# Three couples of chunks per feed-forward stage by seven block products instead of two, with two weight sums made by adding DMA loads and weight units split whole

## The chip, the cores and the metric

One core of a Trainium2 chip runs the whole program. The metric is the device time of one execution in microseconds (us). The engines are called as in the profile: PE (matrix products), PEld (its weight loads), DVE (VectorE), ACT (ScalarE), POOL (GpSimd), SP (which issues DMAs). A change of this kernel's time by less than 0.2% can't be told from none.

## The reference

A decoder trunk of two layers on 256 tokens of 1024 channels in float32. Each layer is a feed-forward step, a mixer of three branches, and a second feed-forward step, each between two RMS norms:

```
for l in range(2):
    h = rms_norm(x, ffn1_pre_g[l])
    x = x + 0.5 * rms_norm(swiglu(h, wi1[l], wo1[l]), ffn1_post_g[l])
    h = rms_norm(x, mix_pre_g[l])
    x = x + rms_norm(hybrid_mixer(h, ...), mix_post_g[l])
    h = rms_norm(x, ffn2_pre_g[l])
    x = x + 0.5 * rms_norm(swiglu(h, wi2[l], wo2[l]), ffn2_post_g[l])

def swiglu(h, wi, wo):                     # wi: 1024 x 5632, wo: 2816 x 1024
    gate, up = split(h @ wi, 2)
    return (silu(gate) * up) @ wo
```

The change lies in the four feed-forward steps (stages, below) and in the way in which all weights are prepared.

## The kernel before

**Weights.** They lie in HBM as units of 128 x 2048 numbers (1 MB), in the order in which they are used. Each product is made of three matmuls (`mm3`, L383 to L385): a weight is split into `hi`, its value rounded to the faster matmul type (ACT, L217), and `lo`, the rest (DVE, L218); likewise the activations (`hh`, `hl`); then hi x hh, lo x hh and hi x hl are added in PSUM. A split is made by halves of a unit, 1024 columns at a time, into a ring of 8 half-units (`RING`).

**Feed-forward stage.** The 2816 hidden columns are 11 chunks of 256 gate and 256 up columns. A chunk needs two units of wi (`c(j, 0)`, `c(j, 1)`, 512 input rows each) and, once its gated product has been transposed, one unit of wo (`w(j)`). In plain form a chunk takes for each of the two token tiles (tt) 8 k-blocks x 3 matmuls of 512 columns, and its wo unit 12 matmuls per tile.

**Couples.** Chunks j and j + 1 with j in `QUADS` are taken together (`pair7`): tokens by input rows by chunks are a 2 x 2 x 2 block product, done by 7 products in place of 8 (the scheme of Strassen and Winograd). It needs sums of the activation blocks (four tiles `sA`, once per stage) and of the weight units: with B11, B21 the two units of chunk j and B12, B22 those of chunk j + 1, the products use B11, T2 = B11 + B12 + B22, B21, T3 = B12 + B22, T1 = B11 + B12, T4 = T2 + B21, B22. They stand in the plan in this order, with two wo units between. Three buffers hold the sums: a (B11, then T1, tile `wa`), b (B12, then T3, `wb`), f (T2, then T4, `wf`); DVE makes them at L226, L227, L231 and L236. With u2, u3 (tile `u`) and the chunks (`cc`), a couple has five post sums of 512 columns on DVE (L536).

**Who sets the order.** The function `trunk` is written as generators with due times (`Clock`): `loader` issues DMA loads on SP, `splitter` emits the splits and sums of `plan` as far ahead as the ring allows, `ffn` and `mixer` emit the matmuls. The framework's scheduler then fixes one order per engine; each engine runs its instructions in this order and waits for semaphores. Streamed units (`raw`) have two buffers, so a load waits until the unit before the last has been split. The tag `q4` has nine buffers of 128 x 1024, for the `sA` tiles, a and b, for tiles of the mixer, and for a few split halves that don't fit in the ring (`place`). The products of a couple write to two PSUM buffers (`mm`). The gated product of a chunk goes ACT (silu), DVE (product), PE (transposes, L330), ACT and DVE (split, L323, L324) and is then used by wo.

Of the kernel before, what the change touches and what calls it, by code (L numbers as in the profile page):

```python
# [9 lines left out]
F32 = mybir.dt.float32  # L10
# [5 lines left out]
P = 128  # L16
# [61 lines left out]
def trunk(ctx, tc, x, wpk, gains, lnp, wst, bst, consts, out, depth=DEPTH):  # L78
# [49 lines left out]
    for l in range(depth):  # L128
        for st0, qj in ((0, QUADS), (33, None), (73, QUADS)):
# [12 lines left out]
            for j in range(2, NCH - 1, 2):  # L142
                if j in qj:
                    k = Quad({}, c(j, 0), c(j, 1), c(j + 1, 0), c(j + 1, 1))
                    if j != qj[0]:
                        k.ffn, k.prev = last.ffn, last
                    else:
                        k.prev = None
# [9 lines left out]
    done, raw = set(), {}  # L158

    def loader():  # L160

        ring = []

        def stream(key, u, first=False):
            while len(ring) >= 2 and ring[-2] not in done:
                yield
            ring.append(key)
            t = rp.tile([P, 2048], F32, tag="raw", name=f"raw{u}", bufs=2)
            raw[key] = [t[:, c] for c in WQ]
            for c in WQ if first else (slice(0, 2048),):  # L170
                load(t[:, c], wpk[u][:, c])

        for n, (kind, k) in enumerate(plan):
            if kind == "w":
                yield from stream(n, k, n == 0)
            elif kind == "B11":
                while k.prev and not k.prev.t1:
                    yield
                f = k.ffn
                if not f:  # L180
                    for t in "ab":
                        f[t] = [sp.tile([P, 1024], F32, tag="q4", name=nm("w" + t), bufs=9) for _ in WQ]
                raw[n] = f["a"]
                for t, u in ((f["a"], k.u11), (f["b"], k.u12)):
                    for q, c in enumerate(WQ):
                        load(t[q], wpk[u][:, c])
                yield from stream(k, k.u22)
            elif kind in ("B21", "B22"):
                yield from stream(n, k.u21 if kind == "B21" else k.u22)
            yield  # L190

    ld = loader()

    def ready(n, kind, k):
        if kind[0] == "T":
            raw[n] = k.ffn[{"T1": "a", "T2": "f", "T3": "b", "T4": "f"}[kind]]
        return n in raw and (kind != "B11" or k in raw)

    def splitter():
        for n, (kind, k) in enumerate(plan):  # L200
            while not ready(n, kind, k):
                next(ld)
            halves[n] = []
            for q in range(2):
                gate = place.get(n)
                while st_["free"] <= 0 if gate is None else not gate.on:
                    yield 0.2
                    gate = place.get(n)
                if gate is not None:
                    h = sp.tile([P, 1024], F32R, tag="q4", name=f"hi{n}_{q}", bufs=9)  # L210
                    lo = sp.tile([P, 1024], F32R, tag="q4", name=f"lo{n}_{q}", bufs=9)
                else:
                    st_["free"] -= 1
                    h = rp.tile([P, 1024], F32R, tag="hi", name=f"hi{n}_{q}", bufs=RING)
                    lo = rp.tile([P, 1024], F32R, tag="lo", name=f"lo{n}_{q}", bufs=RING)
                r = raw[n][q]
                S.copy(h, r)  # L217
                V.tensor_sub(lo, r, f32(h))  # L218
                halves[n].append((h, lo))
                yield 1.2  # L220
            if kind == "B11":
                f = k.ffn
                if "f" not in f:
                    f["f"] = [sp.tile([P, 1024], F32, tag="xn", name=nm("wf"), bufs=2) for _ in WQ]
                for q in range(2):
                    V.tensor_add(f["a"][q], f["a"][q], f["b"][q])  # L226
                    V.tensor_add(f["f"][q], f["a"][q], raw[k][q])  # L227
                    yield 1.2
            elif kind == "T2":
                for q in range(2):  # L230
                    V.tensor_add(k.ffn["b"][q], k.ffn["b"][q], raw[k][q])  # L231
                    yield 0.6
                done.add(k)
# [364 lines left out]
    def mixer(l, gi, nxt):  # L598
# [189 lines left out]
        def branchC():  # L788
            for hp in range(4):
# [240 lines left out]
```

## Time and profile before

| | |
|---|---|
| median of 3 runs | 1264.91 us (1264.59 to 1265.29) |
| profiled execution, own time | 1265.89 us |
| its span | 1263.5 us |
| PE busy | 1248.7 us, granted clock 0.999 of full speed |
| DVE, ACT, POOL busy | 930.6, 701.8, 34.6 us |
| read from HBM | 240.52 MB, 191 GB/s over the span |

The span is the time from the first to the last instruction. Busy time of an engine is the union of its instructions; matmuls overlap, so one that is listed with 390 ns occupies PE for less. The four feed-forward stages end at some 194, 629, 816 and 1263 us; the two mixers lie between 194 and 444 and between 816 and 1066 us.

### The profile page before, as it was taken

The page shows a single profiled execution, that of the slowest core. Times are in us where ns is not written, and L with a number is a line of the kernel's source. Part 1 is how long each engine was busy: PE and PEld are TensorE (multiplying, and loading weights), DVE is VectorE, ACT ScalarE, POOL GpSimd, SP SyncE. Part 2 cuts the span into 40 slices and gives each one's busy share as a digit, 9 for nine tenths or more (in the row PEclk, how much of TensorE's full clock was granted, in tenths as well). Part 3 has the DMA queues.
Part 4 walks back from the last instruction along what each step waited for, and adds up shares of the span by engine and source line. Part 5 has one row for each costly group of instructions (what it writes and reads, how often), then busy time and mean ns, then how long its engine had stood idle before and what let it go on. Part 6 is the DMA issues. An engine that isn't in the chain of part 4 may idle for free.

```text
span 1263.5 us, 16239 instructions
## 1 busy us (share of the span) xinstructions
PE 1248.7 (99%) x6332; PEld 1040.4 (82%) x6332; DVE 930.6 (74%) x1157; ACT 701.8 (56%) x968; POOL 34.6 (3%) x81
## 2 busy tenths in 40 slices
PE   8999999999999999999999999999999999999997
PEld 7788888998778888888888888789977788888886
DVE  5897977646765979878768878765466568798783
ACT  6565665445666555656655646644366655556462
POOL 0000001000000010000000000010000000000000
PEclk9999999999999999999999999999999999999999
DMA  7757465555335545675645665654544355465651
GB/s 250 267 196 294 141 235 178 195 182 192 112 131 200 199 167 200 215 252 170 215 175 197 213 252 192 220 190 163 204 168 134 134 197 200 143 227 208 223 189 63
DMA packets 38381, 242.62 MB, mean 192 GB/s; under 512 B 4512, under 2 KB 4640, under 8 KB 12320
## 3 DMA queue, kind: packets, MB, share of 16 engines
q1 hardware_dynamic: 38304, 241.59, 54.1%
q8 instruction: 49, 0.80, 0.2%
q14 instruction: 28, 0.23, 0.1%
HBM read 240.52 MB, written 1.05 MB: 191 GB/s over the span
## 4 chain that ended last, share of the span: by engine, by line
PE 91%; DVE 4%; DMA 2%; ACT 2%; issue 1%; POOL 0%; SPq 0%; DVEq 0%; POOLq 0%; ACTq 0%
PE mm L383 16%; PE mm L385 16%; PE mm L384 16%; PE acc L385 6%; PE acc L384 6%; PE acc L383 6%; PE qk L384 3%; PE qk L383 3%; PE qk L385 3%; PE tr L330 3%; DMA raw<-wpk 2%; DVE lo L218 2%; PE pj L385 1%; PE pj L383 1%; PE pj L384 1%; ACT hi L217 1%
## 5 line engine op out<-in xcount | busy, mean ns | idle before, releaser
L218 DVE TENSOR_TENSOR lo<-raw,hi 128x1024 fp32r<-128x1024 f32 x392 | 470.2, 1221 | 166.2 <-ACT hi L217 160.8
L217 ACT CAST hi<-raw 128x1024 fp32r<-128x1024 f32 x392 | 402.9, 1049 | 266.2 <-DMA raw<-wpk 72.4
L383 PE MATMUL mm<-hi,hh 128*128 128x512 f32 x864 | 344.8, 399 | 1.1 <-ACT hh L323 1.1
L385 PE MATMUL mm<-hi,hl 128*128 128x512 f32 x864 | 338.4, 392 | 0.2 <-DVE hl L324 0.2
L384 PE MATMUL mm<-lo,hh 128*128 128x512 f32 x864 | 338.3, 392 | 0.0
L383 PEld LDWEIGHTS mm<-hi,hh 128*128 128x128 f32 x864 | 162.8, 188 | 36.0 <-issue 2.7
L385 PEld LDWEIGHTS mm<-hi,hl 128*128 128x128 f32 x864 | 162.6, 188 | 35.5 <-DVE hl L324 0.9
L384 PEld LDWEIGHTS mm<-lo,hh 128*128 128x128 f32 x864 | 163.1, 189 | 30.9
L383 PE MATMUL acc<-hi,gT 128*128 128x512 f32 x352 | 140.5, 399 | 0.0
L385 PE MATMUL acc<-hi,gT 128*128 128x512 f32 x352 | 138.0, 392 | 0.0
L384 PE MATMUL acc<-lo,gT 128*128 128x512 f32 x352 | 137.5, 390 | 0.0
L383 PE MATMUL qk<-hh,hi 128*128 128x256 f32 x320 | 91.3, 285 | 0.0
L385 PE MATMUL qk<-hh,lo 128*128 128x256 f32 x320 | 90.7, 284 | 0.0
L384 PE MATMUL qk<-hl,hi 128*128 128x256 f32 x320 | 90.7, 284 | 0.0
L385 PEld LDWEIGHTS acc<-hi,gT 128*128 128x128 f32 x352 | 66.1, 188 | 13.9
L384 PEld LDWEIGHTS acc<-lo,gT 128*128 128x128 f32 x352 | 66.3, 188 | 12.7
L383 PEld LDWEIGHTS acc<-hi,gT 128*128 128x128 f32 x352 | 66.2, 188 | 12.7 <-ACT gT L323 0.2
L323 ACT CAST gT<-tr 128x256 fp32r<-128x256 f32 x88 | 32.5, 369 | 73.8 <-PE tr L330 73.6
L384 PEld LDWEIGHTS qk<-hl,hi 128*128 128x128 f32 x320 | 61.5, 192 | 0.1
L383 PEld LDWEIGHTS qk<-hh,hi 128*128 128x128 f32 x320 | 61.5, 192 | 0.1
L385 PEld LDWEIGHTS qk<-hh,lo 128*128 128x128 f32 x320 | 61.5, 192 | 0.0
L324 DVE TENSOR_TENSOR gT<-tr,gT 128x256 fp32r<-128x256 f32 x88 | 36.8, 419 | 20.8 <-ACT gT L323 20.1
(170 smaller groups left out, 1552.3 us busy)
## 6 DMA issues: line engine op xcount, KB each, us to landing
raw<-wpk SPq DMA_DIRECT2D x203, 1024.0 KB, 4.9
wa<-wpk SPq DMA_DIRECT2D x16, 512.0 KB, 7.0
wb<-wpk SPq DMA_DIRECT2D x16, 512.0 KB, 8.9
gain<-gains SPq DMA_DIRECT2D x12, 512.0 KB, 7.1
x<-x SPq DMA_DIRECT2D x2, 512.0 KB, 5.6
raw<-wpk SPq DMA_DIRECT2D x2, 512.0 KB, 6.5
ln<-lnp SPq DMA_DIRECT2D x4, 256.0 KB, 5.7
out<-x SPq DMA_DIRECT2D x4, 256.0 KB, 2.0
```

The costliest lines, as they stand in the source:

```text
L217: S.copy(h, r)
L218: V.tensor_sub(lo, r, f32(h))
L323: lasthi[0] = S.copy(h_out, src)
L324: V.tensor_sub(l_out, src, f32(h_out))
L330: T.transpose(tr[:, k * P:(k + 1) * P], src[:, k * P:(k + 1) * P], ident)
L383: T.matmul(o, ah, bh, start=first, stop=False, skip_group_check=go_on)
L384: T.matmul(o, ah, bl, start=False, stop=False, skip_group_check=go_on)
L385: T.matmul(o, al, bh, start=False, stop=stop, skip_group_check=go_on)
```

## The change

Three things change. (1) `QUADS` is (4, 6, 8): three couples in a stage, one directly behind the other. (2) b is now B12 + B22 from the start: B12 is loaded by SP, and POOL issues a DMA that adds B22 to it (`accum_op`); f is a + b; once f is made and B11 split, POOL issues a DMA that adds B12 to a. DVE's sums at L226 and L231 and the second stream of B22 go. b has two sets of buffers, used by couples in turn; half of the second set shares a buffer (`shl`) with two tiles of the mixer that are put into one. The first b of a stage is loaded four plan entries early. (3) A streamed unit in the ring is split whole, 2048 columns in one instruction each on ACT and DVE; the first two units, the sums and the units outside the ring stay halved.

```
-QUADS = (4, 8)
+QUADS = (4, 6, 8)
...
+        def load_b(k):
+            f = k.ffn
+            i = "b" + str(k.par)
+            if i not in f:
+                f[i] = [sp.tile([P, 1024], F32, tag="q4", name=nm("wb"), bufs=9),
+                        sp.tile([P, 1024], F32, tag="shl" if k.par else "q4", name=nm("wb"), bufs=1 if k.par else 9)]
+            k.b = f[i]
+            for q, c in enumerate(WQ):
+                load(k.b[q], wpk[k.u12][:, c])
+            for q, c in enumerate(WQ):
+                nc.gpsimd.dma_start(k.b[q], wpk[k.u22][:, c], accum_op=ALU.add)
...
+            if n + 4 < NI and plan[n + 4][0] == "B11" and not plan[n + 4][1].prev:
+                load_b(plan[n + 4][1])
...
-                for t, u in ((f["a"], k.u11), (f["b"], k.u12)):
-                    for q, c in enumerate(WQ):
-                        load(t[q], wpk[u][:, c])
-                yield from stream(k, k.u22)
+                for q, c in enumerate(WQ):
+                    load(f["a"][q], wpk[k.u11][:, c])
             elif kind in ("B21", "B22"):
                 yield from stream(n, k.u21 if kind == "B21" else k.u22)
+                if kind == "B21" and k.next:
+                    load_b(k.next)
...
+            if gate is None:
+                st_["free"] -= 2
+                ht = rp.tile([P, 2048], F32R, tag="hi", name=f"hi{n}", bufs=RING // 2)
+                lt = rp.tile([P, 2048], F32R, tag="lo", name=f"lo{n}", bufs=RING // 2)
+            if gate is None and n > 1 and n in full:
+                S.copy(ht, full[n])
+                V.tensor_sub(lt, full[n], f32(ht))
+                halves[n] = [(ht[:, c], lt[:, c]) for c in WQ]
+                yield 2.3
...
-                for q in range(2):
-                    V.tensor_add(f["a"][q], f["a"][q], f["b"][q])
-                    V.tensor_add(f["f"][q], f["a"][q], raw[k][q])
-                    yield 1.2
-            elif kind == "T2":
-                for q in range(2):
-                    V.tensor_add(k.ffn["b"][q], k.ffn["b"][q], raw[k][q])
+                for q, c in enumerate(WQ):
+                    V.tensor_add(f["f"][q], f["a"][q], k.b[q])
+                    nc.gpsimd.dma_start(f["a"][q], wpk[k.u12][:, c], accum_op=ALU.add)
                     yield 0.6
...
-                sh = sp.tile([P, 2, 384], F32R, tag="sh", name=nm("sh"), bufs=1)
-                sl = sp.tile([P, 2, 384], F32R, tag="sl", name=nm("sl"), bufs=1)
+                shl = sp.tile([P, 4, 384], F32R, tag="shl", name=nm("sh"), bufs=1)
+                sh, sl = shl[:, 0:2], shl[:, 2:4]
```

How the built order moves is shown at three places of the first feed-forward stage. On POOL, before, the stage's norm at the start is followed at once by that of its end:

```order
L313 TENSOR_SCALAR rs_10_159<-ss_9_149 128x1
L316 TENSOR_TENSOR rs_10_159<-rs_10_159,mh_78 128x1
L313 TENSOR_SCALAR rs_113_1541<-ss_109_1518 128x1
L316 TENSOR_TENSOR rs_113_1541<-rs_113_1541,mh_78 128x1
L313 TENSOR_SCALAR rs_116_1582<-ss_115_1570 128x1
```

On POOL of the change twelve adding loads stand there (`wb_16`, `wb_17` are b of the first and third couple, `wb_48`, `wb_49` of the second, `wa_36` and `wa_37` the halves of a):

```order
L185 DMA wb_16_214<-wpk 128x1024
L185 DMA wb_17_215<-wpk 128x1024
L250 DMA wa_36_374<-wpk 128x1024
L250 DMA wa_37_375<-wpk 128x1024
L185 DMA wb_48_478<-wpk 128x1024
L185 DMA wb_49_479<-wpk 128x1024
L250 DMA wa_36_374<-wpk 128x1024
L185 DMA wb_16_214<-wpk 128x1024
L185 DMA wb_17_215<-wpk 128x1024
L250 DMA wa_37_375<-wpk 128x1024
L250 DMA wa_36_374<-wpk 128x1024
L250 DMA wa_37_375<-wpk 128x1024
```

In the second couple the load into a's second half (`wa_37`) has come to stand behind the two into b of the third couple.

On DVE, before, the sums of the first couple stand so (`wa_29`, `wa_30` are a, `wb_31`, `wb_32` b, `wf_48`, `wf_49` f, `raw15` the first stream of B22):

```order
L226 TENSOR_TENSOR wa_29_377<-wa_29_377,wb_31_379 128x1024
L226 TENSOR_TENSOR wa_30_378<-wa_30_378,wb_32_380 128x1024
L227 TENSOR_TENSOR wf_48_526<-wa_29_377,raw15_436 128x1024
L227 TENSOR_TENSOR wf_49_527<-wa_30_378,raw15_436 128x1024
L231 TENSOR_TENSOR wb_31_379<-wb_31_379,raw15_436 128x1024
L218 TENSOR_TENSOR lo11_0_550<-wf_48_526,hi11_0_549 128x1024
L218 TENSOR_TENSOR lo11_1_561<-wf_49_527,hi11_1_560 128x1024
L231 TENSOR_TENSOR wb_32_380<-wb_32_380,raw15_436 128x1024
```

On DVE of the change the same place in the second couple reads:

```order
L249 TENSOR_TENSOR wf_51_507<-wa_36_374,wb_48_478 128x1024
L249 TENSOR_TENSOR wf_52_508<-wa_37_375,wb_49_479 128x1024
L241 TENSOR_TENSOR lo20_806<-wf_51_507,hi20_805 128x1024
L554 TENSOR_TENSOR cc_73_820<-mm_72_801,u_60_603 128x512
L241 TENSOR_TENSOR lo20_806<-wf_52_508,hi20_805 128x1024
L254 TENSOR_TENSOR wf_51_507<-wf_51_507,raw18_759 128x1024
L554 TENSOR_TENSOR cc_74_840<-mm_67_729,u_60_603 128x512
L488 TENSOR_TENSOR cc_73_820<-cc_73_820 128x256
L229 TENSOR_TENSOR lo21_828<-raw16_711,hi21_827 128x2048
```

Six half-unit sums have become two, the splits of wo and B21 are whole, and the last post sums of the couple before (`cc_73`, `cc_74`) stand between those of the next.

On PE, before, the last product of the first couple (`mm_65`) is followed by a wo unit (`acc`):

```order
L383 MATMUL mm_65_785<-hi18_1_794,sA_42_459 128x512
L384 MATMUL mm_65_785<-lo18_1_795,sA_42_459 128x512
L385 MATMUL mm_65_785<-hi18_1_794,sA_42_459 128x512
L383 MATMUL acc_24_353<-hi19_0_806,gT_64_761 128x512
L384 MATMUL acc_24_353<-lo19_0_807,gT_64_761 128x512
```

On PE of the change the last product of the first couple (`mm_67`) is followed by the first of the second (`mm_76`, which lies in the PSUM buffer of `mm_72`, the product before the last):

```order
L401 MATMUL mm_67_729<-hi18_738,sA_42_429 128x512
L402 MATMUL mm_67_729<-lo18_739,sA_42_429 128x512
L403 MATMUL mm_67_729<-hi18_738,sA_42_429 128x512
L401 MATMUL mm_76_843<-hi19_765,hh_94 128x512
L402 MATMUL mm_76_843<-lo19_766,hh_94 128x512
```

The wo unit has moved behind the second product of the new couple.

## Rows read from the trace of the kernel before

**Rows 1.** The page, busy us (share of span) x instructions, and granted PE clock

```profile
PE 1248.7 (99%) x6332; PEld 1040.4 (82%) x6332; DVE 930.6 (74%) x1157; ACT 701.8 (56%) x968; POOL 34.6 (3%) x81
...
PEclk9999999999999999999999999999999999999999
```

**Rows 2.** Waits of PE, longest first: us in total, times, longest

```profile
PE tr L330 <- DVE sg L443: 3.6, 5, 0.9
PE tr L330 <- DVE xn L351: 1.5, 1, 1.5
PE warm L925 <- POOL ident masks.py:199: 1.4, 1, 1.4
PE mm L383 <- ACT hh L323: 1.1, 1, 1.1
```

**Rows 3.** PE in order of time, second couple: start us, us

```profile
139.55 0.40 PE L385 MATMUL mm<-hi,sA 128*128 128x512 f32 x1
139.78 0.38 PE L330 MATMUL tr<-ident,sg 128*128 128x128 f32 x2
139.92 0.48 PE L383 MATMUL mm<-hi,sA 128*128 128x512 f32 x1
140.24 0.39 PE L384 MATMUL mm<-lo,sA 128*128 128x512 f32 x1
...
142.06 0.39 PE L383 MATMUL acc<-hi,gT 128*128 128x512 f32 x1
...
147.50 0.39 PE L383 MATMUL mm<-hi,hh 128*128 128x512 f32 x1
...
150.22 0.39 PE L383 MATMUL mm<-hi,sA 128*128 128x512 f32 x1
```

**Rows 4.** By stretch: us, busy us of PE, PEld, DVE, ACT, POOL, clock, DMA

```profile
61.00:92.00 31.00, 31.00 (x141) 25.57 (x140) 28.76 (x33) 18.66 (x23) 0.00 (x0) 1.00 0.54 192
...
122.00:153.00 31.00, 31.00 (x141) 25.59 (x141) 29.00 (x32) 17.83 (x22) 0.00 (x0) 1.00 0.48 175
```

**Rows 5.** Groups, DVE and ACT, 122 to 153 us: busy us, mean ns

```profile
L218 DVE TENSOR_TENSOR lo<-raw,hi 128x1024 fp32r<-128x1024 f32 x6 | 7.1, 1218 | 0.1
L236 DVE TENSOR_TENSOR wf<-wf,raw 128x1024 f32<-128x1024 f32 x2 | 2.4, 1220 | 0.4 <-DMA raw<-wpk 0.4
...
L226 DVE TENSOR_TENSOR wa<-wa,wb 128x1024 f32<-128x1024 f32 x2 | 2.4, 1217 | 0.0
...
L536 DVE TENSOR_TENSOR u<-mm,u 128x512 f32<-128x512 f32 x1 | 0.7, 691 | 0.7 <-PE mm L385 0.7
...
L217 ACT CAST hi<-raw 128x1024 fp32r<-128x1024 f32 x7 | 7.3, 1053 | 4.1 <-PE acc L385 1.8 <-PE mm L385 1.3 <-DMA raw<-wpk 0.9
```

**Rows 6.** DVE in order of time, second couple: start us, us

```profile
142.33 0.69 DVE L536 TENSOR_TENSOR u<-mm,u 128x512 f32<-128x512 f32 x1 [0.67 <-PE mm L385]
142.94 1.22 DVE L236 TENSOR_TENSOR wf<-wf,raw 128x1024 f32<-128x1024 f32 x1
144.07 2.35 DVE L218 TENSOR_TENSOR lo<-wb,hi 128x1024 fp32r<-128x1024 f32 x2
146.34 2.35 DVE L218 TENSOR_TENSOR lo<-wa,hi 128x1024 fp32r<-128x1024 f32 x2
...
152.02 0.42 DVE L470 TENSOR_TENSOR sg<-mm,sg 128x256 f32<-128x256 f32 x1
152.35 1.21 DVE L218 TENSOR_TENSOR lo<-wf,hi 128x1024 fp32r<-128x1024 f32 x1
```

**Rows 7.** DMA issues: count, KB, median us to landing; then L115's landings

```profile
raw<-wpk SPq DMA_DIRECT2D x203, 1024.0 KB, 4.9
wa<-wpk SPq DMA_DIRECT2D x16, 512.0 KB, 7.0
wb<-wpk SPq DMA_DIRECT2D x16, 512.0 KB, 8.9
...
DMA to landing us min/median/max: 3.5/5.0/11.0
```

**Rows 8.** DMA from 61 to 92 us in 40 slices: busy tenths, GB/s

```profile
DMA  1000000000009399959999999999996100004699
GB/s 63 11 0 0 0 0 0 0 0 0 0 0 159 137 444 412 285 190 455 370 375 400 411 399 291 217 375 470 402 465 264 53 11 32 0 0 53 95 370 465
```

**Rows 9.** Waits of all engines: us in total, times, longest

```profile
ACT hi L217 <- DMA raw<-wpk: 72.4, 65, 2.8
```

More of the change, by code (lines that the diff above doesn't have):

```diff
@@ L145, in trunk @@
                     if j != qj[0]:
-                        k.ffn, k.prev = last.ffn, last
+                        k.ffn, k.prev, last.next, k.par = last.ffn, last, k, 1 - last.par
                     else:
-                        k.prev = None
+                        k.prev, k.par = None, 0
+                    k.next = None
                     last = k
@@ L157, in trunk @@
     WQ = (slice(0, 1024), slice(1024, 2048))
-    done, raw = set(), {}
+    done, raw, full = set(), {}, {}
     def loader():
@@ L169, in stream @@
             raw[key] = [t[:, c] for c in WQ]
+            full[key] = t
             for c in WQ if first else (slice(0, 2048),):
                 load(t[:, c], wpk[u][:, c])
+        def load_b(k):
[9 more added lines that the diff above has]
+                nc.gpsimd.dma_start(k.b[q], wpk[k.u22][:, c], accum_op=ALU.add)
         for n, (kind, k) in enumerate(plan):
+            if n + 4 < NI and plan[n + 4][0] == "B11" and not plan[n + 4][1].prev:
+                load_b(plan[n + 4][1])
             if kind == "w":
@@ L179, in loader @@
                 f = k.ffn
-                if not f:
-                    for t in "ab":
-                        f[t] = [sp.tile([P, 1024], F32, tag="q4", name=nm("w" + t), bufs=9) for _ in WQ]
+                if "a" not in f:
+                    f["a"] = [sp.tile([P, 1024], F32, tag="q4", name=nm("wa"), bufs=9) for _ in WQ]
                 raw[n] = f["a"]
-                for t, u in ((f["a"], k.u11), (f["b"], k.u12)):
-                    for q, c in enumerate(WQ):
-                        load(t[q], wpk[u][:, c])
-                yield from stream(k, k.u22)
+                for q, c in enumerate(WQ):
+                    load(f["a"][q], wpk[k.u11][:, c])
             elif kind in ("B21", "B22"):
                 yield from stream(n, k.u21 if kind == "B21" else k.u22)
+                if kind == "B21" and k.next:
+                    load_b(k.next)
             yield
@@ L195, in ready @@
         if kind[0] == "T":
-            raw[n] = k.ffn[{"T1": "a", "T2": "f", "T3": "b", "T4": "f"}[kind]]
-        return n in raw and (kind != "B11" or k in raw)
+            raw[n] = k.b if kind == "T3" else k.ffn["a" if kind == "T1" else "f"]
+        return n in raw
     def splitter():
@@ L203, in splitter @@
             halves[n] = []
-            for q in range(2):
+            gate = place.get(n)
+            while st_["free"] < 2 if gate is None else not gate.on:
+                yield 0.2
                 gate = place.get(n)
[L206 to L219, printed above, removed]
-                yield 1.2
+            if gate is None:
[7 more added lines that the diff above has]
+                yield 2.3
+            else:
+                for q in range(2):
+                    if gate is None:
+                        h, lo = ht[:, WQ[q]], lt[:, WQ[q]]
+                    else:
+                        h = sp.tile([P, 1024], F32R, tag="q4", name=f"hi{n}_{q}", bufs=9)
+                        lo = sp.tile([P, 1024], F32R, tag="q4", name=f"lo{n}_{q}", bufs=9)
+                    r = raw[n][q]
+                    S.copy(h, r)
+                    V.tensor_sub(lo, r, f32(h))
+                    halves[n].append((h, lo))
+                    yield 1.2
             if kind == "B11":
@@ L224, in splitter @@
                     f["f"] = [sp.tile([P, 1024], F32, tag="xn", name=nm("wf"), bufs=2) for _ in WQ]
-                for q in range(2):
-                    V.tensor_add(f["a"][q], f["a"][q], f["b"][q])
-                    V.tensor_add(f["f"][q], f["a"][q], raw[k][q])
-                    yield 1.2
-            elif kind == "T2":
-                for q in range(2):
-                    V.tensor_add(k.ffn["b"][q], k.ffn["b"][q], raw[k][q])
+                for q, c in enumerate(WQ):
+                    V.tensor_add(f["f"][q], f["a"][q], k.b[q])
+                    nc.gpsimd.dma_start(f["a"][q], wpk[k.u12][:, c], accum_op=ALU.add)
                     yield 0.6
-                done.add(k)
             elif kind == "B21":
```

## Prediction

> **What bounds the kernel now.** I read the busy times first: TensorE (PE) is busy 1248.7 of 1263.5 us at the full granted clock, VectorE (DVE) 74%, ScalarE (ACT) 56% [rows 1]. A busy PE need not be a fast one, so next the list of what PE waited for: its longest entries are 3.6 us in five waits for a gated activation and 1.1 us, and no split weight (hi, lo) is in it [rows 2]. Then the spacing of matmuls in order of time: the 24 of one wo unit start at 142.06 and the next group at 147.50, so one 512-column matmul costs 5.44/24 = 0.2267 us, back to back, although the row calls it 0.39 us long [rows 3]. PE therefore runs at its own pace from the first chunk to the last, and the time follows the number of matmuls. What can change that is whether splits and sums stay ahead of PE. DVE is nearest: 28.76 and 29.00 us of 31 in the two stretches of the first stage that hold most of its couples [rows 4].
>
> **The change part by part.**
>
> *Products.* A pair of chunks in plain form takes 2 chunks x 2 token tiles x 8 k-blocks x 3 matmuls = 96, a couple 7 x 4 x 3 = 84. One more couple in each of 4 feed-forward stages removes 4 x 12 = 48 matmuls (the built order has 5520 and 5472 of these rows): 48 x 0.2267 = 10.9 us, all on the path, as PE does nothing else meanwhile.
>
> *DVE in a couple.* Before: 18 half-unit splits and 8 half-unit sums. Rows show 1217 to 1220 ns each [rows 5], but two splits start 2.27 us before the next two [rows 6], so one costs 1.135 us. Five post sums of 512 columns cost 142.94 - 142.33 = 0.61 each, eight pieces of 256 columns 152.35 - 152.02 = 0.33 [rows 6]. Sum: 26 x 1.135 + 3.0 + 2.7 = 35.2 us, against PE's 132 matmuls (84 and 48 of two wo units) x 0.2267 = 29.9 plus four pairs of transposes at 0.24 (140.24 - 139.55 less two matmuls), 30.9 us [rows 3]. After: the two sums a+b and b+B22 (four halves) go to adding loads, and four of nine units are split whole. A whole split is not in the trace; from 512 columns (691 ns) to 1024 (1218) is 527 ns [rows 5], so 1024 more columns add 1.05: 2.19 us for 2048, at least 1.135 and at most two halves, 2.27. Sum: 14 x 1.135 + 4 x 2.19 + 3.0 + 2.7 = 30.4 us. A couple goes from 4.3 us over PE to level with it. So three in a row need no more lead than two needed; the removed sums are worth nothing in time themselves, they are what hides the third couple. If that cover is gone, every us over 30.9 lands on PE (second rival).
>
> *ACT.* Its half splits are 1.05 us [rows 5], and in a couple it has 18 to 19 of 31 us to do [rows 4]; whole units shorten that. Cost 0 by itself.
>
> *Whole units as obstacles.* A short operation behind a whole split waits up to 2.19 instead of 1.13 us on DVE, similarly on ACT, and 88 gated activations (22 per stage) pass both on the way to PE's transposes. Five waited before, 3.6 us in all [rows 2]. Bounds: 3.6 us gained (those waits go) to 88 x 1.05 = 92 us lost (each late by a whole remainder). The order was laid anew and puts on average 18.0 instead of 16.6 matmuls between a chunk's end and its transposes, so I stay by the row: +1.5 us. A whole unit is also ready one half later (1.05) and freed 6 matmuls later (1.36); at a stage's end, where units are held through both token tiles, that can bite: 0 to 4 x 2.4 us; PE waited for no split before, so I take +1.5.
>
> *Couple after couple.* No wo unit now stands between the last product of one couple and the first of the next. The first needs the accumulator of the product before the last, so its post sum has 12 matmuls, 2.7 us, of cover; that sum waits for at most one half (1.22) and takes 0.69 [rows 5, 6]. Cost 0, at most 8 places x 0.7.
>
> *First b of a stage.* It is asked for four plan entries early. In the second feed-forward stage of a layer its second half waits on SP for PE's third chunk (which still reads a spare buffer), with the next weight loads behind it. These are loads for units that find no ring slot before the third and fourth chunk end, 5.44 us each, and a load lands in 5.0 [rows 7]: cost 0.
>
> *Adding loads.* Twelve couples x 4 of 512 KB; the trace has none. Bytes: a couple moves 8 units of 1.05 MB, 2 of them adding, in 30.9 us: 272 GB/s as plain loads. The densest slices moved 444 to 470 GB/s [rows 8]; I use 400. Counted once that is 0.68 of the limit, twice 340 GB/s, three times 407, at the limit. Latency: T1's cast waits for the adding load into a. On POOL, in the middle couple, the load into a's second half stands behind two into the next b. From the end of T1's split in the first couple, the next B21 load can leave after DVE has done 7.6 us (two whole splits, two halves, a post, a short piece); behind it the two plain loads of b land 8.9 us later [rows 7], at 16.5. From there to T1's second half the order has two more whole splits, eleven halves, four posts and seven short pieces, 21.6 us: DVE is there at 29.2, and ACT must start 1.05 earlier, at 28.1. That leaves 11.6 us for three adding loads. The quickest load of 1 MB lands in 3.5 [rows 7], of which 1.05/0.4 = 2.6 is transfer, so 0.9 or more is fixed; with the median of 5.0, 2.4. So each may take (11.6 - 2.4)/3 = 3.1 us, against 0.52/0.4 = 1.3 plain: free up to 2.3 times a plain load. Price: 0 below that; at four times, 4 x 3 x (5.2 - 3.1) = 25 us. I take 0, the plain loads being the nearest rows. Behind the waiting cast on ACT stand the next unit's split and a silu, on DVE T1's lo and a post sum, and for these PE waits.
>
> The Trainium skill ("Collectives: The Full Stack", The bandwidth ceiling) says that an add in a DMA needs two source reads on one ring and so runs at half the rate of a copy. By that each takes 2.6 us, inside the 3.1, and the sum stays; no run here shows it. "DMA: Bandwidth & Descriptors" (Issuing engines are not separate DMA queues) adds that POOL's loads share the 16 engines with SP's, which speaks against the change.
>
> *Sum.* The profiled execution took 1265.89 us (span 1263.5), 0.98 above the median of 1264.91. 1265.89 - 10.9 + 1.5 + 1.5 = 1258.0, on the median's scale 1257.0.
>
> **Rivals.**
> 1. *The adding loads are late (slower).* Place: T1 of the middle couple, behind b's loads on POOL. It decides from the point where a stage loses 10.9/4 = 2.7 us, 0.9 per load: 4.0 us each, three times a plain load, where the DMA engines are full too. At four times the 25 us give 1279. For it: DMA landing already ends 72 us of ACT's waits for splits [rows 9], and the order on POOL. Against it: 32% of the transfer rate is free, and elsewhere in a couple the distances are longer.
> 2. *DVE becomes the bound (no change).* In order, DVE also waits for PE and ACT: 2.0 to 2.2 us of each 31 are idle [rows 4]. 30.4 + 2.1 is 1.6 over PE per couple, 4.8 in three. T3's second half was split at 146.42 while PE began that product at 150.22 [rows 3, 6]; its first half had 4.9 us of lead. So the loss about uses up the lead. With 3 us idle per couple the stage loses 3 x 2.5 - 4.9 = 2.6, in all 10.4 us: 1264.4. For it: the tight balance. Against it: before, 35.2 us per couple fitted without a PE wait.
> 3. *All of it and the old waits too.* 1264.91 - 10.9 - 1.5 = 1252.5, if the new order also spares part of the 3.6 us.
>
> **How the numbers follow.** Forecast 0.65, with its own range 1253 to 1262; rival 1: 0.15; rival 2: 0.15, reaching from 1261 to 1272; rival 3: 0.05. Predicted 1257.0. The range 1252 to 1274 leaves out the upper part of rival 1, and a little below. A measurement can tell 0.2%, 2.5 us. Faster: forecast and rival 3 nearly whole, a little of rival 2: 0.71. Same (1262.4 to 1267.4): 0.10, mostly rival 2. Slower: rival 1 and the upper part of rival 2, 0.19.
>
> **What the profile after would show.** Right: 48 fewer product rows at unchanged spacing; PE's list of waits still without hi or lo and under some 8 us; whole splits near 2.28 us long on DVE; ACT's waits for a's adding load near zero. Rival 1: ACT waiting for a DMA into wa at T1, DMA slices full through the couples. Rival 2: PE waiting for hi or lo with DVE over 95% busy in the couples. The forecast is wrong if PE's waits grow by more than 8 us in all, or if matmul spacing itself grows.

## The result: 1.8% slower, and the profile after

| | before | after |
|---|---|---|
| median | 1264.75 us (4 runs, 1264.52 to 1265.29) | 1287.43 us (4 runs, 1284.06 to 1291.41) |
| ratio, 95% interval | | 1.0176 [1.0162, 1.0189] |
| span of the profiled execution | 1263.5 us | 1285.6 us |

The prediction was 1257.0 us, faster: it missed by 30 us and by its sign. The page after answers to [rows 1]; its second line is the clock in 40 slices:

```profile
PE 1247.7 (97%) x6284; PEld 1031.1 (80%) x6284; DVE 932.4 (73%) x1010; ACT 701.5 (55%) x821; POOL 93.8 (7%) x129
...
PEclk8989999999999999999999999999999999999999
```

48 PE instructions are gone, as forecast. They should have taken 10.9 us off PE's busy time, and it fell by 1.0, while idle PE (span less busy time) grew from 14.8 to 37.9 us. So most of the loss is idle PE, and about 10 us are matmuls that took longer or started later by gaps too short to be listed; some 5 us of these were lost at the half clock behind the three longest stalls (an estimate, with its rows in the last section). The 8 in the clock's first slice is no difference: before, too, the matmuls from 12.6 to 14.3 us start 0.43 us apart. The list of PE's waits, which add up to 30.9 us against 8.4, against [rows 2]:

```profile
PE tr L348 <- DVE xn L369: 10.4, 9, 2.6
PE mm L401 <- DVE sg L461: 5.9, 1, 5.9
PE mm L401 <- DVE sg L488: 4.6, 3, 2.5
PE tr L348 <- DVE sg L461: 2.8, 3, 1.9
```

No hi or lo stands among them: split weights are not what is late. Late are gated products (`sg`) and normed activations (`xn`). Of the signs named beforehand, ScalarE's wait for a's adding load near zero and PE's waits under 8 us both failed, and the spacing of matmuls is not unchanged behind a stall.

To see where, I cut the span at the start of every stretch's first product matmul (the built order gives their number: 96 for the first two chunks of a stage, 132 for a couple with its two wo units, and so on) and added up equal stretches, in us until the last product ends. Columns marked "both" have late constants and another POOL order, explained with runs 3 and 4.

| stretch | before | after | halves | halves, both | whole, both | buffers, both | ACT whole, both | DVE whole, both |
|---|---|---|---|---|---|---|---|---|
| 4 x chunks 0, 1 | 106.5 | 111.6 | 108.7 | 107.0 | 112.4 | 108.1 | 112.0 | 111.4 |
| 4 x chunks 2, 3 | 136.8 | 138.2 | 138.7 | 138.2 | 137.9 | 140.0 | 140.1 | 140.0 |
| 4 x first couple | 122.8 | 130.7 | 123.0 | 123.3 | 122.8 | 122.8 | 124.4 | 123.2 |
| 4 x chunks 6, 7 (before plain, then a couple) | 135.8 | 131.7 | 124.8 | 123.8 | 126.6 | 124.7 | 130.3 | 132.1 |
| 4 x last couple | 122.7 | 123.9 | 124.0 | 124.0 | 123.9 | 123.9 | 123.7 | 124.2 |
| 4 x tail | 119.0 | 123.8 | 120.4 | 119.9 | 121.4 | 119.6 | 123.3 | 119.0 |
| 2 x mixer | 513.4 | 519.1 | 513.5 | 513.4 | 519.2 | 515.8 | 518.8 | 515.8 |
| sum | 1257.1 | 1279.0 | 1253.0 | 1249.6 | 1264.1 | 1254.9 | 1272.7 | 1265.7 |

The last couple of a stage, the one that was feared most for VectorE, runs at 31.0 us as planned. Against "halves, both", after loses 4.6 us at the beginnings of stages, 7.4 in the first couples (all of it in the first stage, 38.7 us), 7.9 in the second couples, 3.9 in the tails and 5.7 in the mixers, for which the prediction had no term. Three mechanisms can be seen.

**The constants (first couple of the first stage).** SP issues the loads of the mixer's constant matrices just before POOL's first adding loads into a:

```profile
61.73 1.27 SPq L115 DMA_DIRECT2D cst<-consts  x2
62.09 0.87 POOL L250 DMA_DIRECT2D wa<-wpk  x1 [26.86 <-DVE lo L241]
65.12 0.87 POOL L250 DMA_DIRECT2D wa<-wpk  x1 [2.16 <-issue]
```

VectorE has their casts (L310, L313) in its order ahead of two splits and a gated product, and waits for them (in brackets: idle time before, and its releaser):

```profile
69.13 0.42 DVE L461 TENSOR_TENSOR sg<-mm,sg 128x256 f32<-128x256 f32 x1
75.80 0.56 DVE L310 CAST mB<-cst 128x768 bf16<-128x768 f32 x1 [6.25 <-DMA cst<-consts]
79.20 0.36 DVE L313 CAST mB<-cst 128x384 bf16<-128x384 f32 x1 [2.84 <-DMA cst<-consts]
...
82.21 0.41 DVE L461 TENSOR_TENSOR sg<-mm,sg 128x256 f32<-128x256 f32 x1
```

PE waits for that `sg`, and then its matmuls start 0.43 us apart instead of 0.23; the windows (PE's and the others' busy time, then granted clock, DMA share, GB/s) show the clock at its half level:

```profile
76.36 0.39 PE L403 MATMUL mm<-hi,hl 128*128 128x512 f32 x1
82.68 0.80 PE L401 MATMUL mm<-hi,sA 128*128 128x512 f32 x1 [5.93 <-DVE sg L461]
83.27 0.63 PE L402 MATMUL mm<-lo,sA 128*128 128x512 f32 x1
83.70 0.63 PE L403 MATMUL mm<-hi,sA 128*128 128x512 f32 x1
```

```profile
76.00:82.50 6.50, 0.75 (x4) 0.28 (x2) 3.66 (x6) 1.77 (x3) 0.00 (x0) 0.77 1.04 282
82.50:86.00 3.50, 3.32 (x9) 2.64 (x10) 3.50 (x4) 1.21 (x2) 0.00 (x0) 0.50 0.98 356
```

The DMA engines are full meanwhile, and yet move 225 to 284 GB/s in the slices with adding loads (67 to 80 of the 55 to 85 us shown; most full slices of [rows 8] had 370 to 470):

```profile
DMA  8999970093999998999999999999999999999959
GB/s 251 421 459 453 426 328 11 0 142 131 382 437 377 328 186 208 273 273 262 284 249 270 266 261 256 245 272 268 250 225 241 240 233 242 305 426 432 361 175 415
```

**T1 of the second couples.** ScalarE waits for the adding load into a, 19.8 us in four waits, one per stage, in the place that rival 1 named. In the first stage POOL issues the four loads from 108.36 on (a, two into the next b, a); ScalarE's cast of T1's second half starts at 125.80:

```profile
ACT hi L240 <- DMA wa<-wpk: 19.8, 4, 6.7
```

```profile
108.36 0.87 POOL L250 DMA_DIRECT2D wa<-wpk  x1 [34.90 <-DVE wf L249]
109.66 0.86 POOL L185 DMA_DIRECT2D wb<-wpk  x1 [0.43 <-DMA wb<-wpk]
...
111.72 1.19 POOL L250 DMA_DIRECT2D wa<-wpk  x1
```

```profile
125.80 1.05 ACT L240 CAST hi<-wa 128x1024 fp32r<-128x1024 f32 x1 [6.03 <-DMA wa<-wpk]
```

**Whole splits before short work.** 175 units are split whole, and the duration was forecast well (2288 ns; from the start of one at 79.68 to the next instruction 2.20):

```profile
L229 DVE TENSOR_TENSOR lo<-raw,hi 128x2048 fp32r<-128x2048 f32 x175 | 400.4, 2288 | 178.7 <-ACT hi L228 178.3
L228 ACT CAST hi<-raw 128x2048 fp32r<-128x2048 f32 x175 | 334.3, 1910 | 222.4 <-PE qk L402 65.4
```

At the beginning of the first mixer x is ready to be normed; ScalarE, which has to square it first, is in a whole cast until 213.83:

```profile
212.01 1.91 ACT L228 CAST hi<-raw 128x2048 fp32r<-128x2048 f32 x1 [2.65 <-DMA raw<-wpk]
213.83 0.62 ACT L359 ACTIVATE xn<-x 128x512 f32<-128x512 f32 x1
```

From VectorE's x (start 211.95) to its xn (217.09) it takes 5.1 us; part of it is POOL's small instruction between them, which ends at 216.41, 0.17 us after VectorE's whole split from 213.96 (last section). With halves (run 5) the same chain takes 3.4 us (199.71 to 203.10), and PE, which waits 0.7 us for this xn after the change, doesn't:

```profile
199.49 1.05 ACT L239 CAST hi<-raw 128x1024 fp32r<-128x1024 f32 x1 [1.51 <-DMA raw<-wpk]
200.50 0.63 ACT L360 ACTIVATE xn<-x 128x512 f32<-128x512 f32 x1
```

### The profile page after: what moved, and what is told of

It reads as the page before. It is cut to its first block, busy times and chain, and to the rows that moved or that the text cites. A ratio compares the mean times of both kernels' runs of the same rounds, so it can differ in the third digit from the quotient of the medians.

```text
span 1285.6 us, 15821 instructions
## 1 busy us (share of the span) xinstructions
PE 1247.7 (97%) x6284; PEld 1031.1 (80%) x6284; DVE 932.4 (73%) x1010; ACT 701.5 (55%) x821; POOL 93.8 (7%) x129
## 3 DMA queue, kind: packets, MB, share of 16 engines
q0 software_dynamic: 6912, 25.17, 10.6%
HBM read 257.30 MB, written 1.05 MB: 201 GB/s over the span
## 4 chain that ended last, share of the span: by engine, by line
PE 66%; DMA 12%; DVE 11%; ACT 6%; issue 3%; POOL 2%; SPq 0%; POOLq 0%; DVEq 0%; ACTq 0%
PE mm L401 11%; PE mm L402 11%; PE mm L403 11%; DMA raw<-wpk 7%; DVE lo L229 5%; ACT hi L228 4%; PE acc L402 4%; PE acc L403 4%; PE acc L401 4%; PE qk L402 3%; PE qk L401 3%; PE qk L403 3%; DMA wa<-wpk 3%; PE tr L348 2%; DVE lo L241 2%
## 5 line engine op out<-in xcount | busy, mean ns | idle before, releaser
L229 DVE TENSOR_TENSOR lo<-raw,hi 128x2048 fp32r<-128x2048 f32 x175 | 400.4, 2288 | 178.7 <-ACT hi L228 178.3
L228 ACT CAST hi<-raw 128x2048 fp32r<-128x2048 f32 x175 | 334.3, 1910 | 222.4 <-PE qk L402 65.4
L401 PE MATMUL mm<-hi,hh 128*128 128x512 f32 x784 | 312.4, 398 | 1.1 <-ACT hh L341 1.1
L403 PE MATMUL mm<-hi,hl 128*128 128x512 f32 x784 | 308.2, 393 | 1.5 <-DVE hl L342 1.4
L402 PE MATMUL mm<-lo,hh 128*128 128x512 f32 x784 | 307.6, 392 | 0.0
L401 PEld LDWEIGHTS mm<-hi,hh 128*128 128x128 f32 x784 | 147.7, 188 | 32.4 <-issue 2.0
L402 PEld LDWEIGHTS mm<-lo,hh 128*128 128x128 f32 x784 | 147.8, 189 | 29.3 <-issue 1.0
L401 PE MATMUL mm<-hi,sA 128*128 128x512 f32 x192 | 78.5, 409 | 10.6 <-DVE sg L461 5.9
L403 PE MATMUL mm<-hi,sA 128*128 128x512 f32 x192 | 76.4, 398 | 0.0
L402 PE MATMUL mm<-lo,sA 128*128 128x512 f32 x192 | 76.1, 396 | 0.0
L240 ACT CAST hi<-wa 128x1024 fp32r<-128x1024 f32 x48 | 48.5, 1051 | 34.1 <-DMA wa<-wpk 19.8
## 6 DMA issues: line engine op xcount, KB each, us to landing
gain<-gains SPq DMA_DIRECT2D x12, 512.0 KB, 12.6
```

Source lines behind the costliest of these rows:

```text
L228: S.copy(ht, full[n])
L229: V.tensor_sub(lt, full[n], f32(ht))
L401: T.matmul(o, ah, bh, start=first, stop=False, skip_group_check=go_on)
L402: T.matmul(o, ah, bl, start=False, stop=False, skip_group_check=go_on)
L403: T.matmul(o, al, bh, start=False, stop=stop, skip_group_check=go_on)
```

## The experiments

My theory after the result (A in the expectations) was these three losses side by side. B: the adding loads, by filling the DMA engines, cost all of it. C: VectorE's throughput. All ratios are to the kernel before; since its own median moved from 1264.5 to 1266.1 us between chips, differences are taken between ratios (0.01 is 12.65 us).

**1. Halves.** The splitter's code of before put back into the changed kernel, all else kept; the ring is in half-units again.

```
-                S.copy(ht, full[n])
-                V.tensor_sub(lt, full[n], f32(ht))
...
+                    h = rp.tile([P, 1024], F32R, tag="hi", name=f"hi{n}_{q}", bufs=RING)
+                    lo = rp.tile([P, 1024], F32R, tag="lo", name=f"lo{n}_{q}", bufs=RING)
+                r = raw[n][q]
+                S.copy(h, r)
+                V.tensor_sub(lo, r, f32(h))
```

> The changed kernel with every streamed unit split by halves of 1024 columns again, as before the change; three couples and the adding loads stay. Theory A (three separate losses: whole splits stand as obstacles before short work in the in-order queues, some 13 us spread over mixers, stage beginnings and tails; the constant loads of the first stage come late and block VectorE, 8 us; T1 of the middle couples waits for its adding load, 9 us): the 13 us come back, 1274 us against 1287; the two mixers fall from 259.5 to about 256.7 us each, the stall of some 6 us behind the constants' casts stays. Rival B (the adding loads cost all of it, by filling the DMA engines): no change, 1287 or a little more. Rival C (VectorE is at its limit, and whole splits are what keeps it under): slower than 1287, with TensorE waiting for hi or lo in the couples.

1259.8 us, 0.9961 [0.9946, 0.9976]: 27 us regained, twice what I expected, and faster than before. The two other losses have mostly gone with it: no ScalarE wait for wa is left, VectorE's wait for the constants is 2.0 us, first couples 123.0. But the scheduler laid the orders anew with the halves: POOL now issues both loads into a ahead of those into the next b in all four stages, as run 4 does by an edit, and the constants are asked for later. So the 27 us hold these shifts too. B and C fall. From 92 to 123 us VectorE is busy 30.09 of 31 us and PE loses next to nothing; the second couple of this stage takes 31.7 us:

```profile
92.00:123.00 31.00, 30.91 (x139) 24.85 (x138) 30.09 (x36) 20.70 (x27) 3.48 (x4) 1.00 0.93 267
```

**2. Whole units alone**, put into the kernel before (two couples, sums on VectorE, no adding load).

> The kernel before with only one part of the change, the units in the ring split whole; two couples, sums on VectorE, no adding load. Theory A: slower than 1265 by the same 13 us less what belongs to the third couple, 1273 to 1278, with the loss in the mixers (about 3 us each) and at stage beginnings. Rival B: 1265, nothing happens without adding loads. Rival C: faster or same, since VectorE has less to do: 1262 to 1265.

1280.7 us, 1.0125 [1.0109, 1.0141]: 16 us slower, mixers +6.4, beginnings of stages +5.6, with not one adding load in the program.

**3. Late constants.** `load_consts()` moved behind the first stage's last couple.

```
+            if j == 9 and first:
+                load_consts()
             if j == 4:
-                if first:
-                    load_consts()
```

> The changed kernel with the three constant matrices of the mixer loaded and cast behind the third couple of the first stage instead of in its first couple. Theory A: VectorE no longer waits 6.3 us for them in the first couple, the first couple of the first stage falls from 38.7 to about 31 us, the whole to 1279. Rival B (full DMA engines themselves hold up the weights in that couple): the loss there stays, 1285 to 1287, as a wait for wa, wb or raw. Rival C: no change, 1287.

1277.2 us, 1.0095 [1.0069, 1.0120]: 10 us, as A has it; the first couple takes 30.7 us, the second couples still 130.4 in all.

**4. POOL order.** The adding loads into the next b are issued after T1 of the current couple.

```
             for q, c in enumerate(WQ):
                 load(k.b[q], wpk[k.u12][:, c])
+            if not k.prev:
+                add_b(k)
+
+        def add_b(k):
             for q, c in enumerate(WQ):
                 nc.gpsimd.dma_start(k.b[q], wpk[k.u22][:, c], accum_op=ALU.add)
+
+        st_["add_b"] = add_b
...
             elif kind == "T1":
                 k.t1 = True
+                if k.next:
+                    st_["add_b"](k.next)
```

> The changed kernel with POOL's adding loads in another order: those into the next couple's b are issued only after the current couple's adding loads into a. Theory A: T1 of the middle couples no longer stands behind two adding loads; the second couples fall from 31.4 to 35.4 us towards 31, 5 to 9 us in all, 1278 to 1282; ScalarE's long waits for wa go. Rival B (the adding loads are late by the engines' rate, not by their place in the queue): the waits for wa or wb stay, 1285 to 1290. Rival C: no change, since it is VectorE that is late.

1282.7 us, 1.0137 [1.0120, 1.0153]: 4.9 us, just short of A's 5 to 9. The built orders of PE, ScalarE and VectorE are those of the changed kernel; on POOL both loads into a now go first, ScalarE doesn't wait for them any more, and the second couples fall from 131.7 to 127.4, not to 123:

```profile
109.01 0.87 POOL L256 DMA_DIRECT2D wa<-wpk  x1 [34.61 <-DVE wf L255]
110.14 0.86 POOL L256 DMA_DIRECT2D wa<-wpk  x1 [0.27 <-issue]
110.69 2.11 POOL L189 DMA_DIRECT2D wb<-wpk  x2
```

**5. Halves, late constants and POOL order together.**

> The changed kernel with halves throughout, the constants loaded and cast behind the third couple of the first stage, and the adding loads into the next b issued after those into a. The run with halves alone took 1259.8 us and still has 2 us in the plain chunks of the first stage, 1.1 us before them and 0.3 to 1.0 us in each second couple. Theory A: the constants' 2 us and about half of the second couples' 2.1 us come back, 1256 us. Rival B (the adding loads' traffic costs by itself): 1259 to 1260, unchanged. Rival C (VectorE, with 949 us in all, is at its limit in the third couples): 1259 or more, with the third couples of the stages above 31 us.

1258.2 us, 0.9938 [0.9918, 0.9958]: 7.8 us faster than before, the fastest version that leaves nothing out. It lies between A's 1256 and B's 1259. Against run 1 it is 2.9 us by ratios, no more than the two intervals allow, and POOL's order is the same in both. The second couples take 31.0 us each, so it is the first chunks and the tails that keep it from the forecast 10.9.

**6. Plain loads.** In the changed kernel POOL's loads only copy (`accum_op` taken out, same bytes, buffers and places, and the same built order on every engine); the weight sums are left out.

> The changed kernel with POOL's adding loads made plain loads of the same bytes into the same buffers in the same places (so the weight sums are left out and the output is not the reference's). Theory A (an adding load takes the DMA engines for longer, and this delays the constants and T1): the wait of 6.3 us for the constants and ScalarE's waits for wa (19.8 us in four) shrink to under a quarter, 1270 to 1274. Rival D (the places in the queues do it, whatever the kind of load): 1284 to 1287.

1270.6 us, 1.0036 [1.0022, 1.0051]: the adding itself costs 17.7 us of the changed kernel. Its waits for wa are gone, the one for the constants halved (3.3 us): a middle result there, but D is out. The constants still land 11.0 and 12.0 us after issue, so more of their lateness lies in what is in flight beside them than in the adding. The software queue of the changed kernel (first fence) and of this one carry the same bytes; the last number is the share of 16 engines:

```profile
q0 software_dynamic: 6912, 25.17, 10.6%
```

```profile
q0 software_dynamic: 6912, 25.17, 5.6%
```

10.6% of 1285.6 us is 136 us, 5.6% of 1267.7 is 71: an adding load takes the engines 1.92 times as long. Here the full slices between 55 and 85 us move 312 to 448 GB/s:

```profile
GB/s 453 426 437 426 87 0 44 120 306 448 404 355 328 328 415 404 363 358 393 409 397 418 425 391 312 390 431 410 306 175 191 393 459 371 295 437 382 208 5 191
```

**7. Plain loads under halves**, late constants and POOL order (run 5 without `accum_op`).

> The kernel with halves, late constants and the other POOL order (1258.2 us) with its adding loads made plain loads of the same bytes (the weight sums are left out, so the output is not the reference's). With whole splits the adding cost 17 us. If it costs something here too: 1254 to 1256. If halves, order and constants have hidden it, as the prediction's term of 0 has it: 1257 to 1259.

1256.7 us, 0.9926 [0.9913, 0.9938]: its interval meets that of run 5. Once nothing else is late, the adding costs 1.5 us, which can't be told from nothing. So the 17.7 us of adding and the 27.2 us of whole units overlap: the changed kernel lies 31.6 us above this run, so of their sum, 44.9 us, some 13 count in both.

**8. Two couples with halves and adding loads** (`QUADS = (4, 8)`).

> Halves, adding loads, but two couples a stage as before the change (constants and POOL order as in the changed kernel). If the adding loads are hidden and VectorE was not the limit with two couples: 1264 to 1267, the time before. If a third couple is what the adding loads carry and they cost nothing, this and the run with three couples (1259.8) differ by somewhat less than 10.9 us, 5 to 9. If adding loads cost time by themselves: 1268 or more.

1269.9 us, 1.0030 [1.0020, 1.0041]: 3.8 us above before, so adding loads with all that comes with them (VectorE waits 3.2 us for the constants here) do cost a little; the third couple is worth 8.7 us (against run 1).

**9. Three couples without adding loads.** The kernel before with `QUADS = (4, 6, 8)` and late constants.

> The kernel before (halves, sums on VectorE, no adding load) with one part of the change, three couples a stage; the constants are loaded behind the third couple. 35.2 us of VectorE work a couple stand against 30.9 us of TensorE. If VectorE's lead carries three couples as it carried two: 1254 to 1256, and adding loads were never needed. If VectorE is the bound there (the premise of the prediction): the third couple of each stage takes 4 to 8 us longer, 1265 to 1285, with TensorE waiting for lo.

1311.4 us, 1.0364 [1.0342, 1.0386]. VectorE is the bound, as the prediction's premise had it, and by more than expected: second and third couples take 36.4 to 38.7 us. The window (its fifth entry is VectorE) and the waits:

```profile
92.00:128.50 36.50, 34.89 (x154) 27.46 (x153) 34.53 (x38) 20.36 (x26) 0.00 (x0) 1.00 0.56 191
```

```profile
PE mm L384 <- DVE lo L218: 14.3, 16, 1.8
```

**10. Whole buffers, half instructions.** The ring of the changed kernel stays in whole units, but each is split by two instructions on each engine (the whole branch is never taken).

> The changed kernel with the ring still handed out by whole units (two half slots at once, one buffer of 2048 columns freed at once), but each unit split by two instructions of 1024 columns. It tells which part of whole units costs 27 us: the length of the instruction, or the buffer that is taken and freed whole. If the long instructions do it (short operations wait up to 2.2 us behind them in order, and a unit is ready one half later): near the run with halves, 1260 to 1265. If the whole buffers do it (a split must wait until two slots are free, and holds them until the last half is used): 1280 to 1287.

1266.5 us, 1.0005 [0.9994, 1.0015]. The long instructions make up 21.6 us (by ratios), whole buffers against halves 5.6. Here too POOL issues both loads into a first without an edit, so the 21.6 hold that shift.

**11. Whole on one engine.** First whole casts on ScalarE and halves on VectorE, then the reverse:

```
                 S.copy(ht, full[n])
-                V.tensor_sub(lt, full[n], f32(ht))
+                for c in WQ:
+                    V.tensor_sub(lt[:, c], full[n][:, c], f32(ht[:, c]))
```

> The changed kernel with ScalarE's casts still whole (2048 columns, hi) but VectorE's subtractions (lo) by halves. With whole buffers and halves on both engines the time was 1266.5 us, with whole instructions on both 1287.4. It tells on which engine the long instruction costs those 20.9 us. If on VectorE (2.29 us an instruction, 73% busy, and it carries the post sums, the gated product and the lo half of the activations): 1267 to 1272. If on ScalarE (silu, the hi half of the activations; the first lo also becomes possible one half later): 1280 to 1287. If either alone does it: above 1280 both here and in the twin run.

> The twin: ScalarE's casts by halves, VectorE's subtractions whole. If VectorE's long instruction costs the 20.9 us: 1282 to 1287. If ScalarE's does: 1267 to 1272. If the two add up, each costs some 10 us: 1276 in both.

1289.4 us, 1.0185 [1.0170, 1.0200], and 1280.0 us, 1.0121 [1.0102, 1.0140]. Either alone does it. But the first couple of the first stage took 41.6 and 39.5 us in these two, so the constants stood in the way of a clean answer. It had to be asked again.

**12. The parts of whole units, with late constants and POOL order** (run 5 with whole units; with whole casts only; with whole subtractions only; with whole buffers only).

> The changed kernel, whole units and all, with late constants and the other POOL order: the run with halves in these surroundings took 1258.2 us, so this differs from it by whole units alone. If whole units cost by themselves what they cost the kernel before (16 us) and the three losses add up: 1272 to 1275 (1287.4 less 10.3 for the constants less 4.7 for POOL's order). If they cost mainly through the constants' stall and T1: 1262 to 1267. If they make T1 late whatever POOL's order: 1278 or more.

> As the run before (late constants, other POOL order, whole buffers), with whole casts on ScalarE and halves on VectorE. In the runs so far the mixers took 257.7 us with whole buffers or with whole instructions on VectorE alone, 259.7 with whole ones on ScalarE. If ScalarE's long cast (a gated activation's silu or the activations' hi stands behind it, and lo can start only after the whole of it) is the obstacle: within 2 us of the run with both whole, 1272. If it is VectorE's: 1262 to 1265.

> The twin: halves on ScalarE, whole subtractions on VectorE. If ScalarE's long cast is the obstacle: 1263 to 1267, near whole buffers alone. If VectorE's: 1272. If each costs half: 1267 to 1269 in both.

> Whole buffers, halves on both engines, late constants and the other POOL order. On the changed kernel this gave 1266.5, of which some 3 us are the constants' stall: if the buffers cost the rest, 1260 to 1263; if they cost nothing by themselves, 1258 to 1259.

| against run 5 (0.9938) | us | ratio | costs |
|---|---|---|---|
| whole on both | 1274.6 | 1.0078 [1.0061, 1.0094] | 17.7 us |
| whole buffers | 1263.2 | 0.9985 [0.9973, 0.9996] | 5.9 us |
| and ScalarE whole | 1282.3 | 1.0138 [1.0122, 1.0153] | 19.4 more |
| and VectorE whole | 1272.2 | 1.0060 [1.0045, 1.0075] | 9.5 more |

Without the constants' stall and the late T1, whole units cost what they cost the kernel before (16), give or take some 3 us by the intervals: that much is theirs alone. ScalarE's long cast is the worse of the two: with it the mixers take 519, with VectorE's 516 (whole buffers alone 516). The longest waits of PE, in the order of the table's last two rows, then whole buffers:

```profile
PE tr L357 <- DVE xn L378: 7.8, 8, 1.9
PE mm L410 <- DVE sg L497: 6.3, 5, 1.5
PE tr L357 <- DVE sg L470: 5.4, 8, 0.9
```

```profile
PE mm L410 <- DVE sg L497: 5.1, 3, 2.2
PE tr L357 <- DVE sg L470: 4.9, 5, 2.0
PE tr L357 <- DVE xn L378: 4.6, 3, 1.7
```

```profile
PE tr L356 <- DVE sg L469: 4.9, 6, 2.3
PE tr L356 <- DVE xn L377: 2.0, 2, 1.6
```

And for the norms alone, whole on both against run 5:

```profile
PE tr L356 <- DVE xn L377: 8.0, 9, 1.9
PE tr L349 <- DVE xn L370: 1.7, 1, 1.7
```

ScalarE's variant came out 10 us above the highest time expected for it; VectorE's at the 1272 that was to mean that its long subtraction is the obstacle. So either is one. It is short work in the same queues (norms, gated products) that is late, not weights: none of these lists has a weight's hi or lo. The two don't add up: both whole is 7.6 us better than ScalarE's alone. Each variant has an order of its own, laid by the scheduler for its lengths, and no run keeps the order and changes the lengths alone. So what is shown is the cost of whole units with the order that comes with them; how much of it is the order, and why the pair is milder, stays open.

## Why the prediction was wrong, step by step

*Products, −10.9 us: right.* The stretch of chunks 6 and 7 falls from 135.8 to 123.8 us (run 5), 12.0.

*VectorE in a couple, 30.4 us: right.* Whole splits start 2.20 us before what follows (2.19 was estimated), last couples take 31.0, and run 9 shows what the removed sums are worth: with them on VectorE the four second couples take 148.2 us and the four third ones 153.0, against 124.8 and 124.0 in run 1. Rival 2 did not come.

*Whole units as obstacles, +1.5 and +1.5: the step that failed.* It measured 17.7 us by itself (run 12) and 27.2 in the changed kernel (run 1). Three errors. I took a term from the short end of bounds of −3.6 to +92 and +10, because five waits of 3.6 us in all were the nearest rows; but these rows were so short since nothing long stood in the queues, which the change took away. I counted only the gated activations; the norms at the ends of stages and mixers (`xn`, 10.4 us of waits against 1.5) and the mixers' own short work pass the same queues. And "ready one half later (1.05)" is wrong: the first half is usable after a cast and a subtraction of 1.05 + 1.22 = 2.3 us with halves, after 1.91 + 2.29 = 4.2 when whole, 1.9 later, because the engines no longer overlap within a unit.

*Adding loads, 0: wrong in the changed kernel, nearly right with halves, late constants and POOL order (1.5, run 7).* Rival 1's mechanism came at its very place. From the first load into b to T1's cast are 125.80 − 109.66 = 16.1 us; less the fixed 2.4, that is 4.6 us for each of three loads, beyond the 4.0 from which it was to decide. (The prediction's lower bound for the fixed part, 0.9, was a misreading without effect: the load that landed in 3.5 us was one of x, 512 KB; the quickest of 1 MB took 4.7.) The second couples lost 131.7 − 122.7 = 9 us against the couple's pace before, of which POOL's order gave 4.3 back. What no step had: the loads of the first couple, now with four adding ones among them, fill the engines for *other* loads as well. The constants' two loads landed 14.0 and 16.6 us after issue, against 5.8 and 6.1 before and 11.0 and 12.0 with plain loads (run 6), and their casts, in VectorE's fixed order, held everything behind them; 10 us (run 3). With halves both losses nearly vanish (run 1), by the order laid anew: it asks for the constants 13 us later (74.8 us), behind the four adding loads of that couple, and on POOL it puts both loads into a before those into b.

*Couple after couple, 0:* a couple behind a couple takes 31.0 us, a first one 30.7: 8 x 0.3 = 2.4 us, inside its bound of 5.6.

*ScalarE, 0:* its busy time did not grow (701.8 to 701.5 us), and said nothing about its queue. *The first b of a stage:* not tried by itself.

Summed: of the 30.4 us between forecast and result, 27.2 go with whole units, and 9.5 of these (27.2 − 17.7) are constants and T1, late only beside them and the order that they bring; halves, constants and order together give back 30.1 and leave 1258.2 against the predicted 1257.0. That these two lie so close is partly chance: the 3.0 us that the forecast had for whole units have no place in run 5.

## What to carry to other kernels

A longer instruction on an engine that works in a fixed order is priced by what stands *behind* it: list all short work in that queue that another engine waits for, in every phase, and not only in the phase that the change is about. A list of waits that is short before the change is no price for a change of the lengths that made it short. And a DMA that adds takes the engines twice: look at which other loads are in flight beside it, and who stands behind their consumer.

## What the hardware showed that I had not expected

**POOL is held by VectorE's long subtraction.** The norm's small POOL instruction (128 x 1) takes 0.30 us alone. Beside a split on VectorE it ended 0.17 us after that split in all 20 cases after the change in which it overlapped one, and in all 16 before; the mean went from 524 ns before to 1066. The longest, with the split that holds it:

```profile
826.92 2.28 DVE L229 TENSOR_TENSOR lo<-raw,hi 128x2048 fp32r<-128x2048 f32 x1
```

```profile
827.01 2.36 POOL L331 TENSOR_SCALAR rs<-ss 128x1 f32<-128x1 f32 x1 [2.59 <-ACT xn L359]
```

PE waited 2.6 us behind it (the tail of the third stage, 33.5 us against 30.1). The Trainium skill ("SBUF — State Buffer", SBUF: two separate sides) says that VectorE with two SBUF inputs and a GpSimd instruction that reads SBUF exclude each other for the whole instruction. These rows agree, to the 0.17 us. No run takes this effect away by itself.

**An adding load costs the DMA engines 1.92 plain loads** (run 6). The prediction cited the Trainium skill ("Collectives: The Full Stack", The bandwidth ceiling) for half the rate; the trace agrees. What I made of it was too little: I asked only whether the adding loads themselves would be in time.

**A stall costs more than itself.** After 5.9 us without a matmul, and after stalls of 2.5 and 2.6 us that ended at 758.35 and 830.95 us, the granted clock stood at its half level (1.2 of 2.4 GHz; the first row begins inside the stall, the third before PE starts again):

```profile
79.50:86.40 6.90, 3.72 (x10) 2.94 (x11) 6.79 (x8) 1.32 (x2) 0.00 (x0) 0.51 1.00 348
758.80:762.20 3.40, 3.40 (x11) 2.61 (x10) 3.40 (x4) 1.17 (x2) 0.00 (x0) 0.50 0.88 304
830.50:833.90 3.40, 2.95 (x10) 2.56 (x11) 1.99 (x4) 0.71 (x2) 0.00 (x0) 0.50 0.93 376
```

PE was busy 10.1 us in these three stretches. At the full clock the same matmuls would have taken half of that, so the half clock took some 5 us (an estimate), on top of the 11 us of stalls.
